# Another order of the convolved blocks, and half of the within-chunk part computed beside them

## Chip, core and metric

The kernel runs on one core of one Trainium2 chip. The metric is the device time of one execution in microseconds (us): 1792.51 us before, the median of three runs (1790.63 to 1794.35).

The core has five engines with instruction queues of their own: TensorE (PE) multiplies matrices, VectorE (DVE), ScalarE (ACT) and GpSimd (POOL) work on elements, and SyncE (SP) issues most of the transfers (DMA). A queue is worked off in order; an instruction that waits for a semaphore holds up what stands behind it. A line number such as L924 is a line of the kernel before.

## What is computed

Two layers over 512 latent and 256 context tokens with 1024 channels. Each layer normalises, projects, and runs three mixers on parts of the projection: neighbourhood attention, a bidirectional Mamba-2 scan (SSD) and grouped attention; their outputs are joined, projected and added, and a SwiGLU follows. The change is in the scan, whose heart in the reference is:

```python
a_cum = jnp.cumsum((dt * a).reshape(b, nc, SSD_CHUNK, h), axis=2)
seg = a_cum[:, :, :, None, :] - a_cum[:, :, None, :, :]
decay = jnp.exp(jnp.where(causal, seg, -jnp.inf))
g = jnp.einsum('bcthn,bcshn->bctsh', cr, br) * decay
y_diag = jnp.einsum('bctsh,bcshp->bcthp', g, xr)
...
y = y_f + flip(y_b) + d_skip[:, None] * xs      # then gated by silu(z) and normalised
```

`y_diag` is the part within a chunk of 128 tokens; what enters a chunk from others (`y_off`) is computed apart. In layer 0 all 768 tokens give 6 chunks; in layer 1 only the 512 latent tokens' outputs are needed, 4 chunks. There are 8 heads in two groups of four, g = 0 and 1, so 12 and 8 pairs of chunk and group.

## The kernel before

Channels or tokens lie on 128 partitions. A matrix product in full precision is three products of rounded high and low parts (`wh`, `wl` or `vh`, `vl` for weights; HY, HS, HZ, PHA, PHB for the input). Each layer's first part runs in this order of code:

- `p_kv`, `p_q`: the projections for the grouped attention.
- `p_xbc(b)`, b = 0 to 7: eight **blocks** of 128 channels of x, B and C. PE makes the product in `S` (PSUM, two buffers); ACT and DVE do the convolution of five taps (L768, four DVE steps L773) and the silu (L778, L780, L782). Blocks 0 to 3 are x of both groups, 4 and 5 are B, 6 and 7 are C. Weights (512 KB) come by SP into `wr`, two buffers.
- `p_xtr(b)` (L797, L803): transposes block b to tokens on partitions, by PE and an ACT copy.
- `p_z(g)` (L808): the gate z, one tile of 128 tokens at a time, 24 matmuls (L371) each, stored to DRAM (`zsp`). In layer 0 its tiles stand between blocks and behind the last; in layer 1 all eight tiles stand behind the last block.
- `decays` (L821): the cumulated decays, after block 4; they are stored to DRAM as rows (`crow`), so that they can be loaded again spread over all partitions.
- `mod_steps` (L213): products of the modulation for the next part, one step between other work.

Then comes the **attention stage**: units of scores (L411, L414), softmax on DVE and ACT (exp L431), normalisation on POOL (L437), transposes (L447) with copies (L451, L453) and the product with values (L459). Keys come in the slots KA and KB, two buffers each, with two half loads each (L377); queries in QN. A list of events puts the other work beside the units: *ticks* of the within-chunk part and steps of the scan across chunks (`steps`, L990 to L1011).

`diag(c, g)` (L908) is the within-chunk part of chunk c and group g, a generator of six pieces that the ticks advance; two overlap. It loads two rows of decays, 256 KB each, into `E` (a `wh` buffer) and `Wb` (a `wl` buffer) (L914); ACT adds a bias four times (L920); DVE forms the minimum four times (L924); ACT takes exp (L926); PE multiplies B and C (L929); DVE masks (L931, L932); POOL scales x (L935); DVE multiplies (L939, L940); PE multiplies with x, four heads by two directions (L945, L946); DVE adds the result to `y` (L948), which lies in HY. `skip` (L950) has filled `y` by then with the skip term, 12 POOL instructions (L952) in layer 0 right behind the blocks, 8 in layer 1. y can be made only when the input's HY is no longer read, that is when the last z tile is done.

The order of an engine's queue is the order of this code, but for `tc.issue_after(x)`, which lets instructions of its body be put into the queue behind x.

## Time and profile before

| | |
|---|---|
| median of three runs | 1792.51 us |
| the profiled execution, its own time | 1792.03 us |
| its span, from first to last instruction | 1790.3 us |
| PE busy | 1735.2 us, 97% of the span |
| DVE busy | 1025.0 us, 57% |
| ACT busy | 623.6 us, 35% |
| POOL busy | 265.6 us, 15% |
| layer 0: last four blocks; attention | about 205 to 257; 257 to 417 |
| layer 1: blocks; attention | to about 1225 (z tiles to 1250); 1245 to 1355 |

Rows of the trace are read so. In a table of stretches each engine has its busy time and number of instructions, PEclk is the granted clock of TensorE (1.00 is 2.4 GHz), and the last columns are the share of DMA engines in use and GB/s. In a table of waits each row says which instruction waited for which and for how long in sum. Groups by line give the busy time, the mean duration in ns, and the idle time before. DMA rows give the size and the median time from issue to landing.

### The profile page before, as it was taken

The numbers are of one execution on the slowest core, as the hardware profiler recorded it, in microseconds if no ns is written. First come the engines' busy times: TensorE is split into PE (matmuls) and PEld (weight loads), VectorE is DVE, ScalarE is ACT, GpSimd is POOL, SyncE is SP. The second block draws the span as 40 slices with busy tenths as digits, with TensorE's granted clock in tenths as the row PEclk, the third lists the DMA queues.
The fourth block names the chain that finished last, engine by engine and source line by source line (L and its number), as shares of the span: only waits on it lengthen the run. The fifth ranks groups of instructions, "written<-read, shape, count | busy, mean of one in ns | idle before, by whom it ended". The sixth has DMA issues, their size and how long they took to land.

```text
span 1790.3 us, 26514 instructions
## 1 busy us (share of the span) xinstructions
PE 1735.2 (97%) x10290; PEld 1472.0 (82%) x10290; DVE 1025.0 (57%) x2117; ACT 623.6 (35%) x1202; POOL 265.6 (15%) x289
## 2 busy tenths in 40 slices
PE   7999998999999999999999989999999999999998
PEld 3898886778878888888888878998777888888887
DVE  3645557985575455535554575586895743333335
ACT  4422425665352211221122234334655532232222
POOL 0103116652010000000000011222652100000000
PEclk9999998999989999999999999999999999999999
DMA  9744455522223443333343455233722233333332
GB/s 361 250 130 138 167 159 143 138 89 69 74 86 117 123 121 107 118 105 111 125 122 114 122 162 188 74 108 112 198 63 71 83 107 102 98 93 96 99 106 79
DMA packets 93742, 220.61 MB, mean 123 GB/s; under 512 B 18352, under 2 KB 26160, under 8 KB 93616
## 3 DMA queue, kind: packets, MB, share of 16 engines
q1 hardware_dynamic: 77520, 203.60, 37.3%
q10 hardware_dynamic: 16096, 15.31, 2.6%
q8 instruction: 81, 1.33, 0.3%
q14 instruction: 45, 0.37, 0.1%
HBM read 197.44 MB, written 21.43 MB: 122 GB/s over the span
## 4 chain that ended last, share of the span: by engine, by line
PE 87%; DVE 6%; DMA 3%; ACT 2%; issue 1%; POOL 1%; SPq 0%; ACTq 0%; DVEq 0%; POOLq 0%
PE S L357 66%; PE sm L371 3%; PE PT L371 3%; PE sm L459 2%; PE PT L447 2%; PE PT L357 1%; DMA wr<-in_mod_wT_dram 1%; PE S L411 1%; DVE wh L924 1%; PE S L188 1%; PE S L414 1%; PE PT L188 1%; PE PT L990 1%; PE sm L945 1%; PE sm L946 1%
## 5 line engine op out<-in xcount | busy, mean ns | idle before, releaser
L345 ACT ACTIVATE wh<-wr 128x1024 fp32r<-128x1024 f32 (+2 forms) x204 | 198.0, 972 | 742.6 <-PE S L357 567.0
L346 DVE TENSOR_TENSOR wl<-wr,wh 128x1024 fp32r<-128x1024 f32 (+2 forms) x204 | 227.9, 1118 | 186.4 <-ACT wh L345 184.1
L357 PE MATMUL S<-HY,wh 128*128 128x512 f32 (+1 forms) x716 | 215.9, 359 | 3.9 <-ACT HY L338 3.9
L357 PE MATMUL S<-HY,wl 128*128 128x512 f32 (+1 forms) x716 | 212.5, 354 | 0.3 <-DVE wl L346 0.3
L357 PE MATMUL S<-HZ,wh 128*128 128x512 f32 (+1 forms) x716 | 212.1, 354 | 0.6 <-DVE HZ L339 0.6
L357 PE MATMUL S<-HS,wh 128*128 128x512 f32 (+1 forms) x716 | 211.3, 353 | 0.0
L357 PE MATMUL S<-HS,wl 128*128 128x512 f32 (+1 forms) x716 | 209.3, 350 | 0.0
L286 POOL TENSOR_TENSOR tiny<-tiny,mhalf 128x2 f32<-128x2 f32 (+2 forms) x17 | 27.0, 1590 | 1069.6 <-DVE tiny L1208 1020.6
L245 DVE CUSTOM_DVE_ANT_0 PT<-wr,XFB 128x512 f32<-128x512 f32 x112 | 75.6, 715 | 182.8 <-DMA wr<-in_mod_wT_dram 182.8
L357 PEld LDWEIGHTS S<-HY,wh 128*128 128x128 f32 x716 | 118.7, 191 | 24.0 <-ACT HY L338 4.2
L357 PEld LDWEIGHTS S<-HZ,wh 128*128 128x128 f32 x716 | 118.7, 190 | 22.8 <-DVE HZ L339 2.1
L357 PEld LDWEIGHTS S<-HY,wl 128*128 128x128 f32 x716 | 117.8, 190 | 19.7 <-DVE wl L346 0.6
L357 PEld LDWEIGHTS S<-HS,wh 128*128 128x128 f32 x716 | 116.9, 188 | 18.1
L357 PEld LDWEIGHTS S<-HS,wl 128*128 128x128 f32 x716 | 116.2, 188 | 18.9
L357 PE MATMUL S<-PHA,wh 128*128 128x512 f32 (+1 forms) x358 | 105.6, 352 | 0.0
L357 PE MATMUL S<-PHB,wh 128*128 128x512 f32 (+1 forms) x358 | 104.7, 350 | 0.0
L357 PE MATMUL S<-GX,wh 128*128 128x512 f32 (+1 forms) x400 | 97.7, 350 | 0.4 <-DVE KA L1162 0.4
L437 POOL TENSOR_SCALAR pr<-pr,tiny 128x640 f32<-128x640 f32 (+2 forms) x80 | 72.7, 911 | 98.5 <-DVE tiny L435 89.5
L1309 DVE TENSOR_TENSOR MB<-S,MA 128x768 f32<-128x768 f32 (+1 forms) x42 | 34.6, 824 | 72.0 <-PE S L357 72.0
L357 PEld LDWEIGHTS S<-GX,wh 128*128 128x128 f32 x400 | 65.9, 189 | 11.2 <-DVE KA L1162 0.8
L447 PE MATMUL PT<-c,pr 128*128 128x128 f32 x384 | 65.4, 285 | 9.5 <-POOL pr L437 4.5
L431 ACT ACTIVATE pr<-S,tiny 128x640 f32<-128x640 f32 (+2 forms) x80 | 61.5, 770 | 32.6 <-DVE tiny L424 21.2
(436 smaller groups left out, 3670.1 us busy)
## 6 DMA issues: line engine op xcount, KB each, us to landing
wr<-in_mod_wT_dram SPq DMA_DIRECT2D x56, 512.0 KB, 3.8
wr<-in_w_gate_dram SPq DMA_DIRECT2D x44, 512.0 KB, 3.6
wr<-in_w_up_dram SPq DMA_DIRECT2D x44, 512.0 KB, 3.6
wr<-in_w_blk_dram SPq DMA_DIRECT2D x28, 512.0 KB, 3.8
wr<-in_w_down_dram SPq DMA_DIRECT2D x32, 448.0 KB, 3.4
wr<-in_w_out_dram SPq DMA_DIRECT2D x32, 256.0 KB, 2.8
wr<-in_w_down_dram SPq DMA_DIRECT2D x16, 512.0 KB, 3.5
QN<-in_mod_w_dram SPq DMA_DIRECT2D x24, 256.0 KB, 5.3
```

What stands on the lines that cost most here:

```text
L188: PE.matmul(pm[32 * j : 32 * j + 32, 0:512], lhsT=cs[:, k, :], rhs=w[k], start=(k < 4), stop=(k >= 4), tile_position=(0, 32 * j),)
L245: V.tensor_tensor_reduce(out=ptile() if v == 0 else wv, in0=wv, in1=rows[2 * v + hf], scale=1.0, scalar=0.0, op0=ALU.mult, op1=ALU.add, ac ...
L286: POW.tensor_tensor(out=y, in0=v, in1=mhalf[:, 0:n], op=ALU.pow)
L345: S.activation(hi, raw, AF.Copy)
L346: V.tensor_tensor(lo, raw, hi.bitcast(F32), ALU.subtract)
L357: ins = PE.matmul(pt[:, c0:c1], lhsT=w, rhs=xx[:, c0:c1], start=(k == (0 if len(order) == 1 else order[0]) and i == 0), stop=(k == (nk - 1 ...
L371: PE.matmul(pt[:, 0:n], lhsT=s, rhs=w[:, o : o + n], start=(k == 0 and i == 0), stop=(k == KB - 1 and i == 2),)
L431: exps.append(S.activation(p_, st[:, o0:768], AF.Exp, bias=m[:, 2:3], accum_out=m[:, 3:4]).ins)
L437: G.tensor_scalar(out=p_, in0=p_, scalar1=m[:, 4:5], scalar2=1.0, op0=ALU.mult, op1=ALU.mult).ins
L447: PE.transpose(pt[:, k * P : (k + 1) * P], pr[j, qi][:, kk * P : (kk + 1) * P], ident)
L459: PE.matmul(pv[64 * j : 64 * j + 64, 0:P], lhsT=V2(kts[k], j), rhs=ph[j, qi][:, k, :], start=(k == 0), stop=(k == nkt - 1), tile_position= ...
L1309: V.tensor_tensor(gg[:, c0:c1], pu[:, c0:c1], sg[:, c0:c1], ALU.mult)
```

## The change

Nine of the 20 pairs (c, g), in layer 0 five of the six chunks of group 0 and in layer 1 all four, are done early, beside the last four blocks: `diag(c, 0, True)`. An early diag takes its `E` and `Wb` from the slots KA and KB, which later hold keys, two buffers each. Its result, the skip term included, goes to a `zt` tile and to DRAM (`ysp`), and `load_y` loads it into y at unit 1 of attention. So 7 ticked diags are left in attention of 12 in layer 0, and 4 of 8 in layer 1, over the same units.

For this the blocks run in the order 4, 6, 0, 1, 5, 7, 2, 3, B and C of group 0 and its x first; the decays move ahead of the fifth block. The modulation's weights are loaded to XFB, YO, HD and QN and no longer to KA and KB, and its steps come earlier. In layer 1 six of the eight z tiles go between blocks, and their weights are in `vh` and `vl` in both layers. The transposes of the last block move behind the first z tile after the blocks.

```diff
         def p_z(g):
-            wz = [load_w(..., 1024, "w" if last and g else "v") for i in range(2)]
+            wz = [load_w(..., 1024, "v") for i in range(2)]
...
-        for b in range(8):
-            p_xbc(b)
-            step_md(1)
-            if not last:
-                for _ in range((1, 2, 2, 1, 1, 1, 1, 0)[b]):
-                    next(zs[b // 4])
-                if b == 3:
-                    next(zs[1])
-            if b == 4:
-                dtv, EX, ncum, crow, tdt = decays()
-            if b:
-                p_xtr(b - 1)
...
-        def diag(c, g):
+        def diag(c, g, early=False):
             h0 = 4 * g
-            E, Wb = T(sb, "wh", 3, [P, 4, P]), T(sb, "wl", 3, [P, 4, P])
+            if early:
+                E, Wb = (slot(t, F32, (P, 4, P)) for t in ("KA", "KB"))
+            else:
+                E, Wb = T(sb, "wh", 3, [P, 4, P]), T(sb, "wl", 3, [P, 4, P])
...
+            if early:
+                ydst = T(sb, "zt", 2, [P, 256])
+                skip(c, g, ydst)
+            else:
+                ydst = ysl(g, c)
...
             V.tensor_tensor(ydst, py, ydst, ALU.add)
+            if early:
+                nc.sync.dma_start(ysp[:, c, :], ydst)
...
+        dch = ([4, 5] if not last else []) + [0, 3, 1, 2]
+        ech = dch[0 : 5 if not last else 4]
+        egs = [diag(c, 0, True) for c in ech]
+        et = 0
+        def early(n):
+            nonlocal et
+            for _ in range(n):
+                if et == 0:
+                    next(egs[0])
+                et += 1
+                with tc.issue_after(conv_end[-1]):
+                    for k in range(len(egs)):
+                        if 0 < et - 4 * k < 6:
+                            next(egs[k], None)
+                    if et % 4 == 2 and et // 4 + 1 < len(egs):
+                        next(egs[et // 4 + 1])
+        order = (4, 6, 0, 1, 5, 7, 2, 3)
+        for i, b in enumerate(order):
+            p_xbc(b)
+            step_md(1)
+            if i == 3:
+                dtv, EX, ncum, crow, tdt = decays()
+            if i >= 4:
+                early((2, 2, 2, 2)[i - 4] if last else (2, 3, 3, 3)[i - 4])
+            for _ in range(((1, 1, 1, 1, 1, 1, 0, 0) if last else (1, 2, 2, 1, 1, 1, 1, 0))[i]):
+                next(zs[i // 4])
+            if i == 3:
+                next(zs[1])
+            if i:
+                p_xtr(order[i - 1])
+            if 4 <= i < 7:
+                early(3 if last else (4, 3, 3)[i - 4])
...
+        def load_y():
+            for c in ech:
+                nc.sync.dma_start(ysl(0, c), ysp[:, c, :])
...
-        dgs = [diag(c, g) for c in dch for g in range(2)]
+        dgs = [diag(c, g) for c in dch for g in range(2) if g or c not in ech]
...
-        if last:
-            next(zs[1])
-        else:
-            scores(0)
+        scores(0)
         for n, _ in enumerate(z for g in zs for z in g):
-            if last and n == 5:
-                scores(0)
-            if n == (6 if last else 1):
+            if n == 1:
+                p_xtr(order[-1])
                 scores(1)
```

Three places in layer 0 show what it does to the queues. In the rows the number behind a name is the buffer's; what a row waits for is in brackets (DMAHW is a transfer, Activation is ACT). The line numbers of the changed kernel are a little higher: L413 and L416 are the scores, L799 the transposes of a block, L910 a diag's product of B and C, L931 and L932 its products with x, L373 the z tiles, L359 the blocks, L901 and L905 the bias and the minimum of a diag, L920 and L921 its two multiplications, L933 its sum, L893 its row loads, L379 the key loads.

PE at the end of the blocks, before: the scores follow the last block.

```order
L357 MATMUL S_461_2525<-HS_97_424,wl_460_2522 128x256
L411 MATMUL S_472_2607<-KA_467_2592,QN_466_2589 128x384 [waits DMAHW5_49,DMAHW6_49,DMAHW0_49,DMAHW7_49,DVE_49,Activation_49]
...
L411 MATMUL S_472_2607<-KB_468_2595,QN_466_2589 128x384 [waits DMAHW2_49,DMAHW1_49]
...
L371 MATMUL sm_477_2626<-vh_374_2049,HY_90_417 128x256
...
L411 MATMUL S_481_2684<-KA_467_2592,QN_466_2589 128x384 [waits Activation_49]
...
L411 MATMUL S_481_2684<-KB_468_2595,QN_466_2589 128x384
```

And now:

```order
L359 MATMUL S_488_2661<-HS_97_424,wl_487_2658 128x256
L799 MATMUL PT_496_2745<-c0_66,MB_473_2561 128x128 [waits DVE_49]
L931 MATMUL sm_456_2428<-MA_454_2421,KA_423_2250 128x64 [waits DVE_49,DMAHW2_49,PE_49,Pool_49]
L932 MATMUL sm_456_2428<-MA_454_2421,KB_424_2251 128x64 [waits DMAHW4_49,Pool_49]
...
L799 MATMUL PT_497_2750<-c0_66,MB_473_2561 128x128 [waits Activation_49]
...
L931 MATMUL sm_474_2570<-MA_467_2498,KA_435_2326 128x64 [waits DMAHW7_49,DVE_49,Pool_49]
...
L799 MATMUL PT_515_2854<-c0_66,MB_489_2711 128x128 [waits DVE_49]
...
L931 MATMUL sm_484_2636<-MA_480_2600,KA_462_2487 128x64 [waits DMAHW0_49,DVE_49,Pool_49]
L932 MATMUL sm_484_2636<-MA_480_2600,KB_463_2488 128x64 [waits DMAHW1_49,Pool_49]
...
L910 MATMUL sm_490_2721<-GC_333_1695,GT_312_1561 128x128
L413 MATMUL S_506_2777<-KA_501_2762,QN_500_2759 128x384 [waits DMAHW1_49,DMAHW0_49]
...
L931 MATMUL sm_495_2734<-MA_493_2727,KA_475_2589 128x64 [waits DVE_49,DMAHW5_49,PE_49,Pool_49]
```

Between the last block (S_488) and the first scores (S_506) there now stand transposes, one z tile after another, and the early diags of chunks with the numbers 2, 3 and 4 of the list (sm_456, sm_474, sm_484), each behind transfers into KA and KB; the keys KA_501 are in the buffer that diag 4 (KA_462) had, and the last early diag (sm_495) follows behind the first scores.

SP, before: the row loads of the first diag, then all keys and queries of the first units.

```order
L914 DMA wh_464_2585<-crow_417_2251 128x512 [waits DMAHW3_49,DMAHW2_49,PE_49]
L914 DMA wl_465_2586<-crow_419_2254 128x512 [waits PE_49]
L377 DMA KA_467_2592<-nk_165_727 64x768 [waits DMAHW5_49,PE_49]
...
L377 DMA QN_466_2589<-nq_141_636 64x768 [waits DMAHW7_49,PE_49]
...
L377 DMA KB_468_2595<-nk_167_729 64x768 [waits DMAHW1_49]
...
L914 DMA wh_504_2795<-crow_417_2251 128x512 [waits DMAHW6_49,PE_49]
```

And now:

```order
L893 DMA KA_435_2326<-crow_391_2088 128x512 [waits DMAHW7_49,DVE_49,PE_49]
...
L893 DMA KA_462_2487<-crow_391_2088 128x512 [waits DMAHW0_49,DVE_49,PE_49]
L893 DMA KB_463_2488<-crow_393_2091 128x512 [waits DMAHW1_49,PE_49]
L935 DMA ysp_239_1015<-zt_455_2426 128x256 [waits DMAHW2_49,DVE_49]
L893 DMA KA_475_2589<-crow_391_2088 128x512 [waits DMAHW5_49,DVE_49,PE_49]
...
L935 DMA ysp_239_1015<-zt_468_2503 128x256 [waits DMAHW7_49,DVE_49]
L379 DMA KA_501_2762<-nk_165_727 64x768 [waits DMAHW0_49,DVE_49,PE_49]
L379 DMA KA_501_2762<-nk_165_727 64x768 [waits DMAHW1_49]
L935 DMA ysp_239_1015<-zt_483_2634 128x256 [waits DMAHW2_49,DVE_49]
L379 DMA KB_502_2765<-nk_167_729 64x768 [waits DMAHW3_49,PE_49,Activation_49]
...
L379 DMA KA_504_2771<-nk_165_727 64x768 [waits DMAHW5_49,DVE_49,PE_49]
```

Row loads into KA and KB, the stores of y, and the key loads alternate in one queue; each of them waits for PE's use of the buffer before.

DVE in the last block's convolution, before: softmax steps of the first unit (tiny_473) stand between the four steps of the convolution (MB_462).

```order
L419 ISA S_472_2607,tiny_473_2612<-S_472_2607,GR_474_2613 128x384 [waits DVE_49,PE_49,Pool_49]
...
L773 SCALAR_TENSOR_TENSOR MB_462_2575<-S_461_2525,c1_214,MB_462_2575 128x770 [waits Activation_49]
L424 TENSOR_SCALAR tiny_473_2612<-tiny_473_2612 128x1 [waits DVE_49]
L773 SCALAR_TENSOR_TENSOR MB_462_2575<-S_461_2525,c1_214,MB_462_2575 128x771 [waits DVE_49]
...
L780 SCALAR_TENSOR_TENSOR GC_463_2582<-S_461_2525,MB_462_2575 128x512 [waits Activation_49]
L782 SCALAR_TENSOR_TENSOR GC_463_2582<-S_461_2525,MB_462_2575 128x256
```

And now:

```order
L775 SCALAR_TENSOR_TENSOR MB_489_2711<-S_488_2661,c1_214,MB_489_2711 128x770 [waits PE_49,Activation_49]
L933 TENSOR_TENSOR zt_455_2426<-sm_456_2428,zt_455_2426 128x256 [waits PE_49,Pool_49]
L775 SCALAR_TENSOR_TENSOR MB_489_2711<-S_488_2661,c1_214,MB_489_2711 128x771 [waits DVE_49] x2
L905 SCALAR_TENSOR_TENSOR KA_462_2487<-KA_462_2487,dtr_388_2081,KB_463_2488 128x128 [waits DMAHW1_49,DMAHW0_49,Activation_49]
L775 SCALAR_TENSOR_TENSOR MB_489_2711<-S_488_2661,c1_214,MB_489_2711 128x770 [waits DVE_49]
...
L905 SCALAR_TENSOR_TENSOR KA_462_2487<-KA_462_2487,dtr_388_2081,KB_463_2488 128x128 [waits Activation_49] x3
...
L920 TENSOR_TENSOR KB_436_2327<-KA_435_2326,SB_466_2495 128x512 [waits DVE_49]
L782 SCALAR_TENSOR_TENSOR MB_489_2711<-S_488_2661,MB_489_2711 128x512 [waits Activation_49]
...
L921 TENSOR_TENSOR KA_435_2326<-KA_435_2326,SA_465_2494 128x512 [waits DVE_49]
```

The convolution (MB_489) has the early diags' steps between its own: the sum of diag 2 (zt_455), the minimum of diag 4 (KA_462), which waits for a transfer, and behind it the products of diag 3 (KB_436, KA_435).

## Rows read from the trace of the kernel before

**Rows 1.** The page: busy time, share of the span and instructions of each engine.

```profile
PE 1735.2 (97%) x10290; PEld 1472.0 (82%) x10290; DVE 1025.0 (57%) x2117; ACT 623.6 (35%) x1202; POOL 265.6 (15%) x289
```

**Rows 2.** Table of stretches: blocks, attention of layer 0; blocks, attention of layer 1.

```profile
core 0: us, PE busy (x) PEld busy (x) DVE busy (x) ACT busy (x) POOL busy (x), PEclk, DMA share, GB/s
205.00:257.00 52.00, 51.70 (x328) 45.16 (x329) 26.01 (x40) 16.16 (x29) 7.86 (x8) 0.97 0.64 195
267.00:417.00 150.00, 136.32 (x1051) 108.98 (x1049) 126.19 (x347) 92.89 (x261) 91.38 (x115) 0.97 0.42 119
1100.00:1245.00 145.00, 145.00 (x977) 133.97 (x976) 91.31 (x167) 51.81 (x105) 29.85 (x24) 1.00 0.37 120
1245.00:1355.00 110.00, 102.28 (x797) 81.82 (x796) 97.79 (x251) 67.97 (x175) 69.22 (x82) 1.00 0.48 135
```

**Rows 3.** Table of stretches with gaps of PE; columns as above.

```profile
273.00:285.00 12.00, 8.29 (x39) 6.06 (x41) 9.42 (x20) 4.71 (x12) 8.27 (x9) 0.57 0.11 33
310.00:320.00 10.00, 7.68 (x50) 6.30 (x52) 10.00 (x26) 3.58 (x9) 8.01 (x10) 1.00 0.62 208
```

**Rows 4.** Waits of PE from 250 to 300 us: total us, times, longest.

```profile
PE PT L990 <- ACT PHA L451: 3.2, 1, 3.2
PE S L411 <- ACT pr L431: 2.2, 1, 2.2
PE PT L447 <- POOL pr L437: 0.5, 1, 0.5
```

**Rows 5.** DVE by line in layer 0's attention, then layer 1's; line L948; ACT by line.

```profile
L924 DVE SCALAR_TENSOR_TENSOR wh<-wh,dtr,wl 128x128 f32<-128x128 f32 x48 | 22.6, 505 | 0.5 <-ACT wl L920 0.2
L939 DVE TENSOR_TENSOR wl<-wh,SB 128x512 f32<-128x512 f32 x12 | 9.5, 793 | 0.2
L940 DVE TENSOR_TENSOR wh<-wh,SA 128x512 f32<-128x512 f32 x12 | 9.1, 754 | 0.1
...
L924 DVE SCALAR_TENSOR_TENSOR wh<-wh,dtr,wl 128x128 f32<-128x128 f32 x32 | 19.9, 661 | 0.1
...
L948 DVE TENSOR_TENSOR HY<-sm,HY x20: 407/415/425, 290.6 to 1345.8; 128x256 f32<-128x256 f32 x20
...
L920 ACT ACTIVATE wl<-wl,dtr 128x128 f32<-128x128 f32 x48 | 15.5, 394 | 0.0
```

**Rows 6.** PE in order of time: a diag's first matmul, what follows; two z tiles' first.

```profile
288.65 0.33 PE L945 MATMUL sm<-MA,wh 128*128 128x64 f32 x2
...
290.38 0.50 PE L447 MATMUL PT<-c,pr 128*128 128x128 f32 x3
...
257.44 0.28 PE L371 MATMUL sm<-vh,HY 128*128 128x256 f32 x1
...
260.31 0.28 PE L371 MATMUL PT<-vh,HY 128*128 128x256 f32 x1
```

**Rows 7.** POOL 255 to 300, ACT 205 to 267, DVE's conv step 205 to 257.

```profile
L952 POOL TENSOR_TENSOR HY<-GX,c 128x256 f32<-128x256 f32 x12 | 6.9, 611 | 2.3 <-PE sm L371 2.3
...
L803 ACT ACTIVATE GB<-PT 128x384 f32<-128x384 f32 x4 | 1.9, 490 | 2.0 <-PE PT L797 2.0
...
L773 DVE SCALAR_TENSOR_TENSOR MB<-S,c,MB x12: 1010/1020/1022, 223.2 to 248.8; 128x770 f32<-128x770 f32 x6, 128x771 f32<-128x771 f32 x6
```

**Rows 8.** DMA issues: 225 to 300, then 1225 to 1260, then the page's.

```profile
KA<-nk SPq DMA_DIRECT2D x8, 192.0 KB, 4.3
...
KB<-nk SPq DMA_DIRECT2D x8, 192.0 KB, 4.8
wh<-crow SPq DMA_DIRECT2D x4, 256.0 KB, 3.4
...
KA<-nk SPq DMA_DIRECT2D x4, 192.0 KB, 3.6
...
wl<-crow SPq DMA_DIRECT2D x2, 256.0 KB, 5.0
...
QN<-in_mod_w_dram SPq DMA_DIRECT2D x24, 256.0 KB, 5.3
```

More of the change, by code (lines that the diff above doesn't have):

```diff
@@ L808, in p_z @@
         def p_z(g):
-            wz = [load_w(a["w_z"][l, g, i].rearrange("p k c -> p (k c)"), 1024, "w" if last and g else "v") for i in range(2)]
+            wz = [load_w(a["w_z"][l, g, i].rearrange("p k c -> p (k c)"), 1024, "v") for i in range(2)]
             for t in range(ntt):
@@ L916, in diag @@
             yield
-            with tc.issue_after(exps[-1]):
+            with ExitStack() as q:
+                if not early:
+                    q.enter_context(tc.issue_after(exps[-1]))
                 for h in range(4):
@@ new lines, in hybrid_kernel @@
+        V.tensor_scalar(out=vr, in0=ssr, scalar1=1.0 / 64, scalar2=EPS, op0=ALU.mult, op1=ALU.add)
+        yr = rough(vr, 36)
+        egs = [diag(c, 0, True) for c in ech]
[12 more added lines that the diff above has]
+                        next(egs[et // 4 + 1])
@@ L1092, in hybrid_kernel @@
         dA = [0, 2, 4, 5, 1, 3, 6, 7]
-        dch = ([4, 5] if not last else []) + [0, 3, 1, 2]
-        dgs = [diag(c, g) for c in dch for g in range(2)]
+        dgs = [diag(c, g) for c in dch for g in range(2) if g or c not in ech]
         nd = len(dgs)
```

56 lines of the change are left out of this document (29 added, 27 removed).

## The prediction

> **What bounds the kernel now.** I read the page first, then the table of stretches, then the waits of TensorE, then single lines. The page says that TensorE (PE) is busy 97% of the span [rows 1]. An average hides stages, so the second view is a table of stretches [rows 2]. Where the eight xBC blocks run, PE is full: 51.70 of 52 us in layer 0, 145.00 of 145 in layer 1. In the two attention stages it is not: 136.32 of 150 us and 102.28 of 110. So PE idles 13.7 + 7.7 = 21.4 us there, and VectorE (DVE) is the next fullest engine, 126.19 of 150 (84%) and 97.79 of 110 (89%). PE's work is the same in both kernels, so the time can change only by idle time of PE and by its clock. These 21.4 us are all that the change can win, but for the clock.
>
> Idle time costs clock too: PE worked 8.29 of the 12 us from 273 to 285, behind its first long gap, and the granted clock was 0.57 in the mean [rows 3], near the lower of its two levels (0.50 is 1.2 GHz). Work lost is busy time times the missing share: 8.29 x 0.43 = 3.6 us. The stretch 310 to 320 lost 2.3 us of PE and kept 1.00 [rows 3], so not every gap costs this.
>
> The waits say where layer 0's idle time lies: by 300 us three waits hold 3.2 + 2.2 + 0.5 = 5.9 us [rows 4], a start-up stall of the first softmax chain; the other 7.8 us are many short waits.
>
> **The change, part by part.** *Relief in attention.* A diag, the within-chunk part of one chunk and half of the heads, takes DVE's time by four L924, one each of L939 and L940, two masks (L931, L932) and the sum L948. A mask is half as wide as that sum, 0.28 us as an estimate. By the means of layer 0's attention a diag is 4 x 0.505 + 0.793 + 0.754 + 2 x 0.28 + 0.415 = 4.5 us, in layer 1 with L924 at 0.661 and the other four alike 5.2 us [rows 5]. Five diags leave attention in layer 0 and four in layer 1: 22.7 and 20.7 us of DVE. But PE's part of a diag goes too: 16 matmuls from 288.65 to 290.38, 1.73 us, with the two of L929 2.0 us each [rows 6]. So DVE's share falls only to (126.2 - 22.7) / (150 - 10) = 74% if no idle time went, and 82% if it all did. The end stays a chain of softmax waits with less in their way. I take two thirds of the idle time behind the start-up: 5.2 of 7.8 us in layer 0 and 5.1 of 7.7 in layer 1. POOL's skips ahead of the first normalise fall from 12 to 7, 5 x 0.611 = 3.1 us [rows 7]; the chain goes on through DVE and ACT, so I count half, 1.5 us. Gain: 5.2 + 1.5 + 5.1 = **11.8 us**; bounds 0 (the chain's length stays) and 21.4.
>
> *What goes beside the blocks.* PE is full there, so the 2.0 us of a diag are paid in full; that is the same work as before, at another place, hence 0 in this sum. DVE has 26.01 of 52 us there (50%) in layer 0 and 91.31 of 145 (63%) in layer 1 [rows 2]; four diags of 4.5 us in the 50 us or so of the last four blocks add 36%. That is 86% and 99%: in layer 0 it keeps up, in layer 1 hardly, which is why conv waits stand in that tail below. Bounds: 0 and those waits.
>
> *Layer 0's tail.* Early diags use KA and KB, two buffers each. So the rows of diag 4 can be loaded only when PE has finished diag 2, those of diag 5 after diag 3, and the K of the first scores only after diag 4. Before, that K was loaded while blocks ran. Counting from the last block's last matmul: diag 2 ends at 1.9, SP issues diag 4's two row loads at 2.0 and 2.4, they land 3.4 later [rows 8], at 5.4 and 5.8. ACT then has four L920 (0.394 each [rows 5]) to 7.4 and the PSUM copy L803 (0.49 [rows 7]) to 7.9. PE has done a z tile (24 matmuls, 257.44 to 260.31, 2.87 us [rows 6]) and three transposes by 5.2 and needs that copy: **2.7 us**. DVE's row for diag 4, at 6.7, is put between the last block's conv steps (1.02 us each [rows 7]), so diag 3's products are ready at 12.5, when PE has waited since 11.6: **0.9**. Diag 3 ends at 14.2; its sum, two masks and two products for diag 4 take DVE to 16.6, while PE has transposes to 15.7: **0.9**. Diag 4 ends at 18.3, and only now K is loaded. Between the issue and the first scores PE has one short matmul group, L910. The half K loads (192 KB) took 4.3 and 4.8 us from 225 to 300 and 3.6 from 1225 to 1260 [rows 8]; I take 3.8, since little else is loaded then. With the issue K is there at 22.4, PE arrived at 18.5: **3.9**. The KB of the next scores has diag 5 and five matmuls as cover: **0.3**. Sum 8.7 us. Bounds: 3.3 (K at 3.6 less 0.3, the rest covered) and 11.7 (every landing at 4.3 to 5.0).
>
> *Layer 1's tail.* Before, eight z tiles (23 us) stood behind the last block and covered the first scores. Six of them now go beside blocks, so two are left. By the same way of counting: the weights of the fifth block are issued behind the decays' row store, four row loads and a GR load that waits for PE's L708, **2.5**; the transposes L799 behind a block of 512 tokens need its convolution of four steps, of up to 1.02 us each [rows 7], and its ends, **3.2**; the first K has only diag 3's L910 and one z tile as cover, 1.2, its KB 0.7; L799 needs a conv step that stands behind the first scores' softmax on DVE, 1.4; diag 4 0.6; the second K and KB 0.8 and 1.2. These six are **5.9**. Sum 11.6 us; bounds 2 (landings at 3.6 and DVE never late leave half of the four K waits) and 14.6 (its five waits for a DMA 0.6 longer each).
>
> *Clock.* Layer 0 had its fall already and I let it move ahead. Layer 1 had none from 1245 to 1355 [rows 2], and now has 11.6 us of idle time in some 40: one fall, **3.6 us**; bounds 0 and 7.2.
>
> *Edits at nothing.* The stores of y's half and their loads into HY (128 KB, nine each) are needed many units later, behind which only bias loads queue; if that cover went, one landing, at most the 3.6 us of a larger one [rows 8]. The modulation's loads go to other buffers and a little earlier, beside full PE work; without that cover it is one landing, 5.3 us [rows 8]. The block order alone moves equal work; B and C first is what lets diags run early.
>
> **Sum.** -11.8 + 8.7 + 11.6 + 3.6 = +12.1 us. The profiled execution took 1792.03, so 1804.1; the median of the three runs, 1792.51, is 0.5 higher, and I say **1804**.
>
> A rule on transfers speaks on these tails. The K loads took 3.6 to 4.8 us for 192 KB [rows 8]. The Trainium skill ("DMA: Bandwidth & Descriptors", section "Anatomy of one DMA — SWDGE (gpsimd) path") gives about 2 us fixed plus the bytes at 436 GB/s, an estimate of 2.5 us here, for another issue path. By that the six waits for K, 8.1 us in sum, would shrink to one of 2.6 and the time would be 1798.5; the trace does not agree, and the sum goes by the rows.
>
> **Rivals.** (a) *Faster, 1785.* The relief is as above, 11.8, but the tails cost only their low bounds, 3.3 + 2, and no clock falls: 1792 - 6.5. For it: PE may reach the waiting rows later than I count, since it is full before; each microsecond that it is late shortens a wait. Against it: the K load of layer 0 cannot start before diag 4 is done, and one L910 is all that stands between. It decides from the point where tail stalls and clock together fall below 8 us (11.8 less the 3.6 that a measurement can tell). (b) *No change, 1793.* Tails at half of my count, 10.2 us, with half of the clock, 1.8, cancel the relief: PE may be late for each by as much as it waits. (c) *Much slower, 1817.* All landings at the upper rows, 11.7 + 14.6, and three clock falls, 10.8, less 11.8: +25. For it: 273 to 285 fell behind gaps of this size [rows 3]; against it: 310 to 320 did not. The Trainium skill ("TensorE: Matmul & The Clock Gate", section "HAM oscillation — how this bites in real kernels") describes just this, short bursts of matmuls between waits for DMA, each of which drops the clock anew; the trace agrees at 273 and not at 310.
>
> **How the numbers follow.** The forecast has 0.42, (a) 0.27, (b) 0.13, (c) 0.18. The range reaches from (a) with some 4 us more relief (its bound is 21.4), 1781, to (c) with 3 us for one uncovered landing, 1820; I leave less than 0.2 outside. A measurement here can tell 0.2%, 3.6 us, from no change: faster 0.27, same 0.14, slower 0.59.
>
> **What would show it.** In the profile after: PE idle right behind layer 0's last block, first before L799 by ACT, then some 4 us before the first scores by the DMA into KA; in layer 1 waits of L799 for DVE in the blocks; DVE's share in attention near 75 to 80%; PE idle in attention behind its start-up 2 to 3 us a layer; the clock at 0.5 for a while in layer 1. It is wrong if the K loads land before PE gets there (then (a)), or if the attention stages keep their idle time though DVE has less to do.

## The result and the profile after

The changed kernel takes 1840.70 to 1845.63 us, against 1790.63 to 1794.35 before: a ratio of 1.0283 (95% interval 1.0259 to 1.0306), some 51 us slower. The forecast was 1804 us with a range to 1820. The direction was right and the size was not: four times as much was lost as was forecast, and the time lies beyond the range and beyond the rival (c), 1817. A fourth execution of the changed kernel took 4330 us and is left out of these numbers. The profiled execution took 1845.63 us with a span of 1843.8.

The page of the changed kernel, its first line as in [rows 1]:

```profile
PE 1756.2 (95%) x10290; PEld 1486.7 (81%) x10290; DVE 1020.6 (55%) x2117; ACT 626.6 (34%) x1202; POOL 258.4 (14%) x289
```

The number of PE's instructions is the same as before. PE's busy time rose by 1756.2 - 1735.2 = 21.0 us for the same work, and its idle time from 1790.3 - 1735.2 = 55.1 to 1843.8 - 1756.2 = 87.6 us, by 32.5. The sum is the 53.5 us by which the span grew.

Where they lie is seen when both kernels are cut at their first scores and at the last product with values of each layer. The idle time of PE, and the work that the clock lost (busy time times the share missing from the granted clock), summed over stretches of 1 us:

| stage | length before, after | idle before, after | lost to the clock before, after |
|---|---|---|---|
| layer 0, from 150 us to the first scores | 106.9, 135.5 | 1.2, 14.7 | 1.7, 4.5 |
| layer 0, attention | 169.0, 168.4 | 13.7, 18.5 | 3.5, 9.6 |
| layer 1, from 1093 (1122 after) to the first scores | 138.8, 169.3 | 0.0, 11.9 | 0.0, 3.4 |
| layer 1, attention | 133.5, 127.4 | 7.9, 9.8 | 0.0, 4.4 |

The clock's columns account for 16.7 of the 21.0 us of busy time. Both block stages grew by some 30 us, and the attention stages, out of which nearly all of the nine diags went, got shorter by 0.6 and 6.2 us only, though one z tile of layer 0 and three of layer 1, 2.9 us each, also stand ahead of the cut now. The stretches of the changed kernel that hold most of it, columns as in [rows 2]:

```profile
210.00:220.00 10.00, 5.87 (x38) 5.09 (x38) 2.53 (x6) 4.34 (x12) 0.00 (x0) 0.92 0.89 299
260.00:270.00 10.00, 5.59 (x46) 5.16 (x45) 5.90 (x12) 4.03 (x10) 1.80 (x3) 0.98 0.43 119
280.00:290.00 10.00, 6.92 (x33) 6.66 (x32) 3.74 (x9) 1.91 (x5) 1.96 (x3) 0.50 0.35 93
330.00:340.00 10.00, 0.96 (x12) 0.58 (x8) 1.66 (x3) 1.10 (x3) 1.85 (x2) 0.73 0.79 225
340.00:350.00 10.00, 9.56 (x41) 8.85 (x42) 6.54 (x21) 3.83 (x13) 5.71 (x7) 0.59 0.26 88
1230.00:1240.00 10.00, 3.17 (x20) 2.64 (x20) 2.97 (x5) 5.25 (x13) 1.75 (x2) 0.78 0.74 271
...
1290.00:1300.00 10.00, 5.67 (x25) 5.04 (x24) 5.58 (x15) 3.20 (x7) 2.77 (x5) 0.68 0.23 72
```

Against the full block stages of [rows 2] PE has only 5.87 of 10 us from 210, 5.59 from 260 and 3.17 from 1230; in attention it has 0.96 from 330. In or behind each of these the granted clock falls to the lower of its two levels, 0.50 (1.2 GHz), for some 3 to 14 us by stretches of 1 us, which the rows above show as means of 10 us.

The longest new or grown waits of PE in the whole changed kernel, columns as in [rows 4]:

```profile
PE S L413 <- ACT pr L433: 12.1, 6, 9.3
PE S L359 <- ACT wh L347: 11.9, 4, 6.6
...
PE PT L799 <- ACT GX L805: 4.5, 2, 3.9
PE S L413 <- DMA KA<-nk: 4.3, 2, 3.1
...
PE PT L799 <- DVE GT L782: 3.0, 1, 3.0
PE S L413 <- DMA KB<-nk: 2.8, 2, 1.8
```

L359 is the blocks' matmul, waiting for ACT to round weights, most of all ones that have only just come; L799 are the transposes of a block; L413 the scores, first for the softmax before and then for keys. Why the weights came late is told by SP's queue (start, duration, line, transfer):

```profile
204.68 1.30 SPq L863 DMA_DIRECT2D crow<-SA  x2
...
208.59 0.34 SPq L893 DMA_DIRECT2D KA<-crow  x1
209.03 0.39 SPq L893 DMA_DIRECT2D KB<-crow  x1
209.46 0.44 SPq L893 DMA_DIRECT2D KA<-crow  x1
210.00 0.38 SPq L345 DMA_DIRECT2D wr<-in_w_blk_dram  x1
```

The weights of the fifth block (wr) stand behind the store of the decays' rows (crow) and among the row loads of the first two early diags. They start at 210.00. PE has a z tile to do until 214 and then idles, in layer 0 for 3.58 us and in layer 1 for 6.62 (in brackets):

```profile
217.64 0.61 PE L359 MATMUL S<-HY,wh 128*128 128x512 f32 x2 [3.58 <-ACT wh L347]
...
1239.09 1.01 PE L359 MATMUL S<-HY,wh 128*128 128x512 f32 x2 [6.62 <-ACT wh L347]
```

In the chain of the changed kernel (start, duration) they take 6.08 us, and further on stand one row load, one load of keys, and a store of 128 KB with 13.54 us:

```profile
210.00 6.08 DMA wr<-in_w_blk_dram
...
261.89 4.68 DMA KB<-crow
...
282.01 3.37 DMA KA<-nk
...
325.53 13.54 DMA ydr<-SB
```

In layer 1 the same weights take 9.14 us:

```profile
1228.81 9.14 DMA wr<-in_w_blk_dram
```

The page of the kernel before has these weights at 3.8 us in the median, and from 200 to 225 us they take longer. The four row loads of 256 KB, queries and weights are under way at once:

```profile
wr<-in_w_blk_dram SPq DMA_DIRECT2D x28, 512.0 KB, 3.8
...
wr<-in_w_blk_dram SPq DMA_DIRECT2D x4, 512.0 KB, 6.3
...
KA<-crow SPq DMA_DIRECT2D x2, 256.0 KB, 4.0
KB<-crow SPq DMA_DIRECT2D x2, 256.0 KB, 5.4
```

How much of that the row loads bring is told by the run without early diags, below.

### The profile page after: what moved, and what is told of

It reads as the page before. It is cut to its first block, busy times and chain, and to the rows that moved or that the text cites. A ratio compares the mean times of both kernels' runs of the same rounds, so it can differ in the third digit from the quotient of the medians.

```text
span 1843.8 us, 26555 instructions
## 1 busy us (share of the span) xinstructions
PE 1756.2 (95%) x10290; PEld 1486.7 (81%) x10290; DVE 1020.6 (55%) x2117; ACT 626.6 (34%) x1202; POOL 258.4 (14%) x289
## 4 chain that ended last, share of the span: by engine, by line
PE 85%; DVE 5%; DMA 5%; ACT 2%; issue 1%; POOL 1%; SPq 0%; ACTq 0%; DVEq 0%; POOLq 0%
PE S L359 64%; PE sm L373 3%; PE sm L461 3%; PE PT L373 3%; PE PT L449 2%; PE PT L359 1%; PE S L413 1%; DMA wr<-in_mod_wT_dram 1%; PE sm L932 1%; PE sm L931 1%; DMA wr<-in_w_blk_dram 1%; PE S L416 1%; PE PT L188 1%; DMA ydr<-SB 1%; PE S L188 1%
## 5 line engine op out<-in xcount | busy, mean ns | idle before, releaser
L348 DVE TENSOR_TENSOR wl<-wr,wh 128x1024 fp32r<-128x1024 f32 (+2 forms) x202 | 226.6, 1122 | 204.6 <-ACT wh L347 202.2
L359 PE MATMUL S<-HY,wh 128*128 128x512 f32 (+1 forms) x716 | 214.4, 357 | 14.7 <-ACT wh L347 10.5
L359 PE MATMUL S<-HY,wl 128*128 128x512 f32 (+1 forms) x716 | 214.9, 358 | 0.3 <-DVE wl L348 0.3
L359 PE MATMUL S<-HZ,wh 128*128 128x512 f32 (+1 forms) x716 | 212.8, 355 | 1.1 <-DVE HZ L341 1.1
L359 PE MATMUL S<-HS,wl 128*128 128x512 f32 (+1 forms) x716 | 211.1, 353 | 0.0
L359 PE MATMUL S<-HS,wh 128*128 128x512 f32 (+1 forms) x716 | 209.0, 350 | 0.0
L359 PEld LDWEIGHTS S<-HY,wh 128*128 128x128 f32 x716 | 119.9, 192 | 36.8 <-ACT wh L347 11.1
L359 PEld LDWEIGHTS S<-HZ,wh 128*128 128x128 f32 x716 | 118.3, 191 | 21.0 <-DVE HZ L341 1.7
L359 PEld LDWEIGHTS S<-HY,wl 128*128 128x128 f32 x716 | 119.1, 192 | 19.9 <-DVE MA L338 0.8
L359 PEld LDWEIGHTS S<-HS,wh 128*128 128x128 f32 x716 | 117.2, 188 | 19.9
L359 PEld LDWEIGHTS S<-HS,wl 128*128 128x128 f32 x716 | 116.9, 188 | 18.2
L359 PE MATMUL S<-PHA,wh 128*128 128x512 f32 (+1 forms) x358 | 105.2, 351 | 0.0
L359 PE MATMUL S<-PHB,wh 128*128 128x512 f32 (+1 forms) x358 | 104.6, 350 | 0.0
L359 PE MATMUL S<-GX,wh 128*128 128x512 f32 (+1 forms) x400 | 98.1, 351 | 0.4 <-DVE KA L1202 0.4
L439 POOL TENSOR_SCALAR pr<-pr,tiny 128x640 f32<-128x640 f32 (+2 forms) x80 | 67.9, 851 | 67.3 <-DVE tiny L437 42.6
L359 PEld LDWEIGHTS S<-GX,wh 128*128 128x128 f32 x400 | 66.3, 190 | 11.5 <-DVE KA L1202 0.8
L433 ACT ACTIVATE pr<-S,tiny 128x640 f32<-128x640 f32 (+2 forms) x80 | 61.6, 771 | 34.4 <-DVE tiny L426 22.6
L775 DVE SCALAR_TENSOR_TENSOR MB<-S,c,MB 128x770 f32<-128x770 f32 (+3 forms) x64 | 62.9, 983 | 17.8 <-ACT MB L770 16.7
```

Source lines behind the costliest of these rows:

```text
L348: V.tensor_tensor(lo, raw, hi.bitcast(F32), ALU.subtract)
L359: ins = PE.matmul(pt[:, c0:c1], lhsT=w, rhs=xx[:, c0:c1], start=(k == (0 if len(order) == 1 else order[0]) and i == 0), stop=(k == (nk - 1 ...
L433: exps.append(S.activation(p_, st[:, o0:768], AF.Exp, bias=m[:, 2:3], accum_out=m[:, 3:4]).ins)
L439: G.tensor_scalar(out=p_, in0=p_, scalar1=m[:, 4:5], scalar2=1.0, op0=ALU.mult, op1=ALU.mult).ins
L775: V.scalar_tensor_tensor(ac[:, s0:s1], pt[:, s0 + j - 2 : s1 + j - 2], convw[l][:, b, j : j + 1], ac[:, s0:s1], ALU.mult, ALU.add,)
```

## The experiments

All runs with the ratio to runs of the kernel before on the same chip, 95% intervals, and what the ratio makes of 1790 us:

| run | what | ratio | us |
|---|---|---|---|
| the change | | 1.0283 (1.0259 to 1.0306) | +50.7 |
| b_nod | before, nine diags left out | 0.9918 (0.9894 to 0.9943) | -14.7 |
| b_dvm | before, DVE's steps of these nine left out, all but the sum | 0.9975 (0.9964 to 0.9987) | -4.5 |
| b_dve | before, one DVE step of each diag three times | 1.0175 (1.0159 to 1.0191) | +31.3 |
| b_ord | before, block order alone | 1.0038 (1.0023 to 1.0053) | +6.8 |
| b_ordd | the same, decays earlier | 1.0027 (1.0013 to 1.0042) | +4.8 |
| a_noe | the change, early diags left out | 1.0013 (0.9998 to 1.0029) | +2.3 |
| a_nozl | the same, layer 1's z tiles behind the blocks | 0.9986 (0.9974 to 0.9999) | -2.5 |
| a_w5 | the change, fifth block's weights early | 1.0148 (1.0118 to 1.0177) | +26.5 |
| a_lz | the change, z loads at unit 18 | 1.0234 (1.0213 to 1.0256) | +41.9 |
| a_w5lz | both | 1.0121 (1.0103 to 1.0138) | +21.7 |
| a_zt | the change, early results in own buffers | 1.0290 (1.0273 to 1.0307) | +51.9 |
| a_w5zl | weights early, layer 1's z tiles behind the blocks | 1.0164 (1.0149 to 1.0179) | +29.4 |
| a_w5e | weights early, five early diags and not nine | 1.0071 (1.0056 to 1.0086) | +12.7 |

### What attention can give: the diags left out, lightened, and made heavier

The first run takes the nine diags out of the kernel before and puts nothing elsewhere:

```diff
-        dgs = [diag(c, g) for c in dch for g in range(2)]
+        dgs = [diag(c, g) for c in dch for g in range(2) if g or c not in dch[0 : 4 if last else 5]]
```

> The kernel before with the within-chunk part of group 0 left out for the nine pairs that the change does early (it is in no output). This is the relief that attention can get at all, with nothing put beside the blocks. PE loses 9 x 2.0 us of work. If attention hangs on DVE (23 + 21 us less of it), PE's idle time there falls from 21 to about 10 us as well: 1791.6 - 18 - 11 = about 1763 us. Rival, attention hangs on the softmax chains and not on DVE's load: only the work of PE goes, 1774 us or a little less.

It gained 14.7 us (10.2 to 19.0), no more than the 18 us of PE's work that are gone. The forecast had counted 18 + 11.8. The 18 are the prediction's 2.0 for each diag; in the profiled execution, which at 1781.94 us was 7 us slower than the median, PE's busy time fell by 12.5 and its idle time rose by 2.3:

```profile
PE 1722.7 (97%) x10128; PEld 1455.1 (82%) x10128; DVE 998.8 (56%) x2036; ACT 609.7 (34%) x1157; POOL 244.3 (14%) x271
```

Two more runs take DVE alone. One keeps PE's work of the nine diags and leaves out DVE's steps but the sum:

```diff
+            lean = not g and c in dch[0 : 4 if last else 5]
-            for h in range(4):
+            for h in range(0 if lean else 4):
                 ...  # the minimum
-            S.activation(E, E, AF.Exp)
+            S.activation(E, E, AF.Exp if not lean else AF.Copy)
...
+            if not lean:
                 ...  # both masks
+            if not lean:
                 ...  # both multiplications
```

> The kernel before, in which the nine pairs' diags keep their loads, ACT, POOL and PE instructions and leave out DVE's steps (minimum, masks, both multiplications; exp becomes a copy), so that some 38 us leave DVE in attention and nothing leaves PE. Without the diags altogether 15 us were gained, 18 of PE's work gone; with 30 us more on DVE 31 were lost. If less DVE work is worth something by itself, this gains 8 us or more. If PE and the chains take over at once, it is within 4 us of the kernel before.

It gained 4.5 us. The bounds of the expectation were 4 and 8, so this is next to nothing, but not nothing. The other one adds to DVE:

```diff
-            V.tensor_tensor(Wb, E, gl..., ALU.mult)
+            for _ in range(3):
+                V.tensor_tensor(Wb, E, gl..., ALU.mult)
```

> The kernel before with one multiplication of each diag (L939, about 0.75 us) issued three times, which changes no result: 40 more instructions, some 30 us more for DVE in the two attention stages and nothing for PE. If attention hangs on DVE's load, as the prediction counted, it costs 15 us or more, 1805 us and up. If it hangs on chains of short waits with DVE's load beside them, under 8 us.

It lost 31.3 us. The two attention stages of the kernel before, columns as in [rows 2], cut at the first scores and the last product with values:

```profile
256.85:425.88 169.03, 155.35 (x1188) 126.31 (x1187) 136.55 (x377) 104.17 (x291) 97.25 (x124) 0.97 0.40 116
1231.85:1365.39 133.54, 125.64 (x985) 102.67 (x984) 105.24 (x273) 77.47 (x201) 75.20 (x90) 1.00 0.42 118
```

Without the nine diags:

```profile
253.40:419.72 166.32, 148.95 (x1098) 117.51 (x1097) 122.91 (x332) 96.61 (x266) 85.58 (x114) 0.97 0.35 102
1228.48:1354.99 126.51, 120.22 (x912) 95.86 (x911) 93.64 (x237) 71.79 (x181) 68.13 (x82) 0.99 0.39 108
```

Without DVE's steps of them:

```profile
253.99:419.26 165.27, 155.13 (x1189) 127.74 (x1187) 123.18 (x337) 103.18 (x290) 94.23 (x124) 0.97 0.41 119
1223.40:1357.88 134.48, 127.89 (x985) 104.57 (x984) 92.92 (x241) 76.85 (x200) 71.82 (x90) 0.97 0.42 117
```

With DVE's added steps:

```profile
253.69:443.15 189.46, 164.54 (x1189) 135.94 (x1187) 156.66 (x401) 105.51 (x291) 103.19 (x124) 0.90 0.35 104
1249.72:1395.07 145.35, 131.51 (x985) 106.75 (x984) 116.76 (x289) 78.59 (x201) 76.54 (x90) 0.95 0.38 109
```

DVE's time grows by 20.1 + 11.5 = 31.6 us where steps are added, and the time by the same, so attention does hang on DVE. That the two are equal is chance: PE idles 24.9 and 13.8 us where it had 13.7 and 7.9, 17.2 more, and the other half is the clock, 0.90 and 0.95 in the mean and no longer 0.97 and 1.00, at which the same matmuls are busy for 15.1 us more. But where DVE's steps go, 13.4 + 12.3 = 25.7 us of them, PE's idle time falls only from 13.7 to 10.1 in layer 0 and from 7.9 to 6.6 in layer 1. And where the diags go as a whole, PE's idle time in layer 0 rises to 17.4, and the stage is only 2.7 us shorter for the 10 us of PE's work that left it; in layer 1 idle time falls to 6.3, and the stage is 7.0 us shorter for 8. It looks as if the diags' matmuls had filled gaps that the chains of softmax steps leave. More work for DVE costs there, less of it is worth little; what more work for PE alone would cost, no run shows.

The terms of the sum were also too high: DVE's busy time lost 25 us with the diags, where 43 had been counted by the mean durations. One reason is that durations overlap: in layer 0's attention before, those of all DVE instructions add up to 160.6 us where the busy time is 136.55 (in [rows 5], 48 x 0.505 = 24.2 us of L924 are 22.6 us busy). So the busy time falls by less than the lengths that go. Another, smaller one, in layer 0, is seen in the L924 that stay:

```profile
L924 DVE SCALAR_TENSOR_TENSOR wh<-wh,dtr,wl 128x128 f32<-128x128 f32 x28 | 16.1, 609 | 0.6
```

Their mean is 609 ns, higher than the 505 of [rows 5] with all diags. In the kernel before the line's shortest, median and longest were 328, 356 and 1611 ns:

```profile
L924 DVE SCALAR_TENSOR_TENSOR wh<-wh,dtr,wl x80: 328/356/1611, 272.8 to 1336.2; 128x128 f32<-128x128 f32 x80
```

A few long ones raise the mean, and in layer 0 many of these stay when the others go.

### The new order without early diags

```diff
             nonlocal et
-            for _ in range(n):
+            for _ in range(0):
...
-                    if g or c not in ech:
-                        skip(c, g, ysl(g, c))
+                    skip(c, g, ysl(g, c))
```

> The changed kernel without its nine early diags (left out with their loads, stores and the loads of y; the skip goes to y directly). The order of the blocks, the decays before the fifth block, the z tiles and the seven and four ticked diags stay. Theory, the early diags with their transfers bring the 50 us: this kernel comes within 5 us of the kernel before without the same diags. Rival, the new order itself (decays and z weights ahead of the fifth block's weights, z tiles no longer behind the blocks) costs: it stays 15 to 30 us above that.

It was as slow as the kernel before (+2.3 us) with nine diags less, 17.0 us over the kernel before without the same diags. So the rival holds: a third of the loss has nothing to do with early diags as such.

This run also shows what the row loads do to the fifth block's weights. In its chain, with no row load in front of them, these take, in layer 0 and layer 1:

```profile
208.58 6.00 DMA wr<-in_w_blk_dram
...
1199.38 5.70 DMA wr<-in_w_blk_dram
```

With row loads it was 6.08 and 9.14. So in layer 1 the landing is 3.4 us longer with the row loads. In layer 0 it only starts 1.4 us later with them; what else is under way there, queries and stores, is enough for 6 us. PE waited here for these weights 0.7 us in layer 0 and 0.3 in layer 1, not 3.6 and 6.6.

Part of the 17.0 us came back with layer 1's z tiles behind the blocks:

```diff
-                for _ in range(((1, 1, 1, 1, 1, 1, 0, 0) if last else (1, 2, 2, 1, 1, 1, 1, 0))[i]):
+                for _ in range(((0,) * 8 if last else (1, 2, 2, 1, 1, 1, 1, 0))[i]):
...
             if n == 1:
                 p_xtr(order[-1])
+            if last and n == 5:
+                scores(0)
+            if n == (6 if last else 1):
                 scores(1)
```

> The changed kernel without its early diags (left out as in the run without them), and with layer 1's eight z tiles behind the blocks again, five of them ahead of the first scores. Theory, the z tiles between the blocks cost layer 1 their cover: PE idle there falls by 6 to 7 us, 1784 us. Rival, the cost sits in the new block order and in the early decays: it stays at 1790 to 1792.

4.8 us, somewhat less than expected, and the first scores of layer 1 again stand behind five z tiles. Then the block order alone, in the kernel before:

```diff
-        for b in range(8):
+        order = (4, 6, 0, 1, 5, 7, 2, 3)
+        for i, b in enumerate(order):
             p_xbc(b)
...
-                p_xtr(b - 1)
+                p_xtr(order[i - 1])
```

> The kernel before with nothing changed but the order of the blocks (4, 6, 0, 1, 5, 7, 2, 3; the transposes of the last block then stand behind the first z tile after the blocks). The changed kernel without early diags is as slow as the kernel before though 18 us of PE work are missing, 13 to 17 more than without the new order. If the block order does that, this costs 5 us or more; if not, it is within 3 us of the kernel before.

6.8 us. The prediction had the order itself at nothing, but one wait that comes of it, 3.2 us for a convolution, it had counted in layer 1's tail. This wait stands in layer 1's block stage, where PE of the kernel before waited for nothing:

```profile
PE PT L797 <- DVE GT L780: 3.5, 1, 3.5
```

The blocks 6 and 7, which are 512 wide in layer 1, stand in the middle now. The transposes of a long block come behind one of these short ones, before the convolution on DVE has ended. The decays' place by itself costs nothing more:

```diff
-            if i == 4:
+            if i == 3:
                 dtv, EX, ncum, crow, tdt = decays()
```

> As the run with the block order alone, and with the decays ahead of the fifth block as in the changed kernel (no early diags, z tiles and modulation as before). If the decays' place delays the fifth block's weights by itself, without row loads, it costs 5 us or more over the run with the block order alone; if the row loads of the early diags are what the weights stood behind, within 3 us of it.

4.8 us, within the noise of the run with the order alone. The store of the decays, without row loads behind it, does not hold up the weights by an amount that can be measured. Of the 17.0 us then 6.8 are the order, 4.8 layer 1's z tiles, and 5.4 are not settled (the modulation's place; in layer 0 one z tile less stands behind the first scores).

### The fifth block's weights

```diff
             if i == 3:
+                pre[order[4]] = load_raw(wsrc(6 + order[4]), 1024)
                 dtv, EX, ncum, crow, tdt = decays()
```

Here `load_raw` is the first half of `load_w`, the allocation of wr and the transfer, and the fifth block uses what it left.

> The changed kernel with the load of the fifth block's weights issued ahead of the decays, so that it is ahead of the row store and of the row loads on SP. In the changed kernel PE waits for them from 207 to 218 and from 1231 to 1238, about 16 us, and the clock falls behind. Theory, that wait is one cause by itself: both waits go and with them some clock, 16 to 22 us, 1820 to 1826 us. Rival, the next wait (convolution, early diags) takes the place: less than 6 us gained.

1817 us, 24.2 less than the changed kernel, the most that any single edit gave back that leaves no work out. In the run SP issues that transfer 60 us earlier:

```profile
149.58 0.86 SPq L345 DMA_DIRECT2D wr<-in_w_blk_dram  x2
```

(two blocks' weights, the fifth's the second) and PE goes on where it idled in the changed kernel:

```profile
205.00:215.00 10.00, 10.00 (x64) 8.93 (x64) 3.95 (x6) 4.75 (x12) 0.00 (x0) 1.00 0.82 229
215.00:225.00 10.00, 8.11 (x57) 7.18 (x56) 5.35 (x7) 5.04 (x10) 1.62 (x1) 1.00 1.00 302
```

What is left from 215 to 225 (1.89 us) is the sixth block's weights, which now wait behind the row loads. The gain is a little over the theory's upper end of 22, but not for its reason alone: the expectation put the two waits at about 16 us, and they are 3.6 + 6.6 = 10.2. By the two profiles PE idles 17.8 us less in all (69.8 for 87.6), and its busy time is 8.7 us shorter (1747.5 for 1756.2). So more than half of the gain is what follows from late weights, in the clock and in later waits.

### The other suspects

The z loads at a later unit:

```diff
-        ev.append((14, 2, load_z))
+        ev.append((18, 2, load_z))
```

> The changed kernel with the loads of z (four of 384 KB) at unit 18 of layer 0's attention and not at unit 14. In the changed kernel ACT waits 8.9 us there for a store of 128 KB (ydr) that takes 13.5 us among these loads and the key loads; the clock falls behind it. Theory, this collision is a cause by itself: 9 to 13 us gained, 1829 to 1833 us. Rival, keys and queries of the next units are late anyhow and hold the same units: less than 4 us gained.

8.8 us gained (50.7 - 41.9), just under the theory's lower end of 9. The store that ACT waited for, in the changed kernel (who waited, us, times; landings of its ten transfers):

```profile
  ACT SB L646: 8.9, 1
...
DMA to landing us min/median/max: 1.7/3.3/13.5
```

and with the z loads later:

```profile
  ACT SB L646: 1.4, 1
...
DMA to landing us min/median/max: 1.7/3.6/6.3
```

Whether this is a cause beside the weights was tried with both edits:

> The changed kernel with both single edits, the fifth block's weights ahead of the decays (26 us faster by itself) and the loads of z at unit 18 (7 to 9 faster by itself). If the collision of the z loads with the key loads has a cause of its own, the two add: 1808 to 1810. If it is a consequence of the late weights (the units after them meet the loads), the second edit gives nothing more: 1814 to 1820.

1811.9 us, 4.8 under the weights alone, with intervals that overlap (1.0103 to 1.0138 against 1.0118 to 1.0177). It lies between the two outcomes: of the 8.8 us about half is left. Part of the collision followed from the late weights (with the weights alone in time the longest of these stores takes 9.3 us and ACT waits 3.4); how large the share that did not is, is not settled.

The buffers of the early results:

```diff
-                ydst = T(sb, "zt", 2, [P, 256])
+                ydst = T(sb, ("YO", "HD")[ech.index(c) % 2], 1, [P, 512])[:, 0:256]
```

> The changed kernel with the early diags' results in buffers of their own (YO and HD, free at that time) and no longer in the two zt buffers that the z tiles use. In the chain of the changed kernel the z stores stand three times with 1.7, 3.1 and 4.1 us between 270 and 301. Theory, the shared buffers tie the early diags to the z stores: these go, 5 to 9 us gained with layer 1, 1833 to 1838 us. Rival, the key loads behind them end later than that anyhow: within 3 us of the changed kernel.

Nothing was gained (1.0290 against 1.0283). The chain had named the z stores three times, but when they are gone PE waits for DVE's multiplications of the same diags (L931 for L921), and then for the keys as before:

```profile
PE sm L931 <- DVE KA L921: 3.9, 2, 2.6
...
PE S L413 <- DMA KA<-nk: 3.2, 1, 3.2
```

Layer 1's z tiles behind the blocks, with early diags and early weights (the first scores stand behind five of them, as above):

```diff
                 pre[order[4]] = load_raw(...)
...
-                for _ in range(((1, 1, 1, 1, 1, 1, 0, 0) if last else (1, 2, 2, 1, 1, 1, 1, 0))[i]):
+                for _ in range(((0,) * 8 if last else (1, 2, 2, 1, 1, 1, 1, 0))[i]):
```

> The changed kernel with the early diags, with the fifth block's weights ahead of the decays, and layer 1's z tiles behind the blocks. From 1817 with the weights alone. Theory, the z tiles cover the key loads and the transposes of the last blocks: layer 1's idle time falls by some 8 us and 2 us of clock, 1806 to 1809 us. Rival, the early diags' own steps on DVE hold layer 1's blocks: 1814 us or more.

1821, not better than the weights alone. So the rival holds with early diags on board: now the transposes (L806 here) wait in the blocks themselves for DVE, which has the diags' steps between its convolutions, and there is no z tile to do meanwhile:

```profile
PE PT L806 <- DVE GT L789: 7.0, 2, 3.5
...
PE PT L806 <- DVE MB L789: 3.8, 2, 2.4
```

With the weights alone in time these two rows had 3.1 and 1.3 us.

Last, fewer early diags:

```diff
-        ech = dch[0 : 5 if not last else 4]
+        ech = dch[0 : 3 if not last else 2]
```

> The changed kernel with the fifth block's weights ahead of the decays and only five early diags (three and two of the nine); the other four are ticked in attention as in the kernel before. With nine 1817, with none 1792 (but nine diags left out). If each early diag costs its PE work and nothing is won in attention, the ticked ones cost the same: 1810 to 1816. If the loss sits at the end of the blocks, where the last early diags hold KA and KB before the keys, most of the 27 us over the kernel before goes: 1800 or less.

1803.7, 13.8 us less than with nine. That lies between the two expectations: four diags back in attention give 13.8 us, 3.4 each, more than the 2.0 us that each costs PE, and about half of the loss that was left. No run beat the kernel before but those that leave work out.

## Why the prediction was wrong

The runs make a way from the kernel before to the changed one, each step a difference of two ratios times 1790 us. The nine diags leave attention: -14.7. The new order, without early diags: +17.0. The early diags beside the blocks, weights in time: +24.2; by the two profiles PE's busy time is 22.4 us longer (1747.5 for 1725.1), of which 4.5 are lost to the clock and some 18 are the diags' work, and its idle time 1.7. The weights behind the row loads, with what follows from that: +24.2. Sum 50.7. By the intervals of its two ends each step is uncertain by 4 to 7 us, and taken in another order the steps could be of other sizes.

**Relief (-11.8, with PE's moved work at 0).** This step failed: no relief came. The prediction had named the sign itself, attention stages that keep their idle time though DVE has less to do. In the changed kernel these two stages are, cut and columns as above:

```profile
285.52:453.92 168.40, 149.86 (x1088) 121.33 (x1089) 113.66 (x327) 94.62 (x263) 84.24 (x111) 0.93 0.37 109
1291.29:1418.65 127.36, 117.52 (x860) 92.47 (x861) 91.24 (x236) 71.67 (x179) 70.38 (x84) 0.96 0.41 108
```

DVE's share fell to 67% and 72%, below the 75 to 80% that had been forecast, and PE idles 18.5 and 9.8 us where it had 13.7 and 7.9. Nor does leaving the diags out give any relief: 14.7 us (10.2 to 19.0) came out of attention for the 18 us of PE's work that went into the blocks in full, which is something between 1.0 us won and 7.8 lost, where 11.8 won had been forecast. The bounds named 0 as the worst case, "the chain's length stays". But a stage that keeps its length while 18 us of PE's work leave it gives nothing back, and the blocks take 18 us more; so the worst case was a loss of 18. DVE's share had been read as room to win. The added DVE work shows that DVE does bind, 17.2 us more of idle time for 31.6 us of work; the removed one, 4.5 us for 25.7, that it is not alone. The relief in DVE's time was also mis-sized, 25 us and not 43.

**Layer 0's tail (8.7).** In the changed kernel this came out, partly by luck. From 260 to 290 PE idled 4.4 + 1.7 + 3.1 = 9.2 us, with the two waits named first: L799 for ACT's copy 3.9 in its longest (2.7 forecast), the first keys 3.1 (3.9 forecast). In the chain stand the row load into KB and the load into KA that the prediction had named. But the prediction had counted with the fifth block's weights in time. In the run where they are, this tail lies from 255 to 285, and neither of these two waits appears; PE idles 0.1 us to 265 and then 2.5 + 1.3, 3.9 in sum:

```profile
265.00:275.00 10.00, 7.46 (x48) 7.26 (x49) 8.06 (x14) 3.94 (x9) 1.08 (x2) 0.83 0.64 196
275.00:285.00 10.00, 8.74 (x48) 8.28 (x47) 3.92 (x14) 2.64 (x6) 6.96 (x9) 0.68 0.45 127
```

**The weights (2.5 in layer 1, nothing in layer 0).** This step failed in its size. The mechanism was named for layer 1; in layer 0 the transfers ahead of the weights had been put at nothing. PE waited 6.6 us in layer 1 and 3.6 in layer 0, 10.2 where 2.5 had been counted, and weights in time were worth 24.2 us, half of the loss. In layer 1 the landing grew, 9.14 us with the row loads and 5.70 without them; in layer 0 it did not, and the transfer was only issued later. The other 14.0 us are what followed: the clock behind these waits, and waits that are not there when the weights are in time, as in layer 0's tail. How these hang together is not settled.

**Layer 1's tail (3.2 + 5.9).** This held. The convolution wait was 3.0 us. It belongs to the block order, as the run with the order alone shows (3.5 us there). Of the six others PE waited 1.3 us for the first keys, 1.8 and 1.0 for those in KB, and 1.3 before L799, 5.4 in sum, most of it in the row from 1290 to 1300.

**Clock (3.6).** This step failed in its size. 21.0 us of busy time were added for the same work, 16.7 of them found in stretches with a lower granted clock, over four times as much. One fall more had been forecast, and three in the rival (c); in the four stages the granted clock fell to 0.50 eight times, and twice before. The row from 310 to 320 in [rows 3] was given too much weight: its 2.3 us of idle time are several gaps, the longest of 1.3 us. The gaps of 3 to 9 us here all had a fall in or right behind them: 0.50 from 280 to 290, at the wait for the first keys, and 0.59 from 340 to 350, behind the wait for a store. The Trainium skill ("TensorE: Matmul & The Clock Gate", section "HAM oscillation — how this bites in real kernels") describes this for short bursts of matmuls between waits for DMA, and this trace agrees with it at these two waits.

**Edits at nothing.** The block order cost 6.8 us, of which 3.2 had been counted as the convolution wait. Layer 1's z tiles between the blocks cost some 4.8, and had no term but the cover that they took from the tail. The collision of the z loads with keys and a store, 8.8 us by itself, was not seen. The prediction looked at each queue's order and not at how fast the units would run on: before, keys and queries were loaded from 291 to 301 and z from 309, and in the changed kernel keys, z and queries all from 318 to 332.

## What to carry to other kernels

Moving work out of a stage in which the bottleneck engine has gaps into one in which it is full costs that work, unless the first stage gets shorter by as much; the test is to leave the work out first, before finding it a new place, and see what the stage gives back. That the next engine is busy 84 to 89% of a stage, as DVE was here, says that more work for it may cost, and not what less would bring. When transfers are put into a queue ahead of others, look for the first urgent one behind them, and price it with what else is under way then, and with the clock that the wait costs. A term that comes out as forecast while another is wrong may do so by luck: measure it with the other one mended.

## What was not expected of the hardware

A transfer of 512 KB, 3.8 us in the median, took 9.14 us in layer 1 beside four loads that spread a row over 128 partitions, and 5.70 without these four; in layer 0 it took 6.08 us with them and 6.00 without. A store of 128 KB took 13.54 us while some 4 MB of loads were under way, and 6.3 at most when 1.5 MB of them were issued four units later.
